# Projecting the first 128 rows un-normalised, from a copy laid out by feature, and applying the norm's factor when the result is evacuated

## The chip, the core and the metric

The kernel runs on one NeuronCore of a Trainium2 chip. The metric is the device time of one execution in microseconds (us), the median of several. The core has five engines with a queue of instructions each: PE (matrix multiply), DVE (vector), ACT (scalar and activation), POOL (GpSimd) and SP (which here only issues DMAs). An engine takes its queue strictly in order; an instruction that waits for a semaphore holds back all that stand behind it. PE writes into PSUM, which this kernel uses as eight banks of 128 x 512 floats.

## The reference, cut to what matters

Four layers, each `x += norm(mixer(norm(x)))` and then `x += norm(swiglu(norm(x)))`, over 512 prompt rows and 128 sample rows of width 1024. The change lies at the very start, in the first mixer's v projection:

```python
def rms_norm(x, g):
    y = xf * lax.rsqrt(jnp.mean(xf * xf, axis=-1, keepdims=True) + EPS)
    return (y * g.astype(jnp.float32)).astype(x.dtype)
...
hp = rms_norm(xp, norm_mix_pre[layer])
...
proj = h @ w_in
u, v, bg, cg, xb = jnp.split(proj, [...], axis=-1)
...
mu = jnp.mean(vf, axis=-1, keepdims=True)
var = jnp.mean(jnp.square(vf - mu), axis=-1, keepdims=True)
vn = ((vf - mu) * lax.rsqrt(var + EPS) * v_gain.astype(jnp.float32)).astype(v.dtype)
```

The norm of a row is one factor s for that row times a gain per feature. A product with un-normalised rows (gain applied, factor not) is therefore v / s, its mean is mu / s and its variance var / s².

## The kernel before

The 640 rows are five tiles of 128 (t = 0 to 4, here x0 to x4). All matrix products are made in split precision: an operand is a high part (ACT copies it to fp32r) and a low part (DVE subtracts the high part from it), written by `split`, and each product is three matmuls. A weight is loaded into a `raw` buffer (two buffers, two weights each) and split into a `q` tile by `operand`.

At the start `main` (L1259 on) loads x0, the gain (a broadcast to 128 partitions, L200), the first two v weights, x1, and the last two v weights. For each tile `pre_norm` (L352) squares the rows with a sum on ACT, makes mean and power −0.5 on DVE and POOL (L234), scales the rows with DVE, transposes them by eight PE transposes ("flips", L171) into two PSUM banks, and `Quarters.take` (L317) writes the splits (`x2`, `x3`, `a11`, `a12` and so on, high by ACT and low by DVE), plain copies `f` of the top half by ACT, and for the lower half a number of sums and differences, each split again. `v_proj` (L418) then makes 24 matmuls of 512 columns for each tile, in one bank `ps`, and `v_evac` in `even_mixer` (L711) evacuates it: BN_STATS, BN_AGGR, an addition, the power on POOL and one more instruction on DVE give a scale and a shift, and ACT writes the normalised rows `vn` from the bank, which is free from then on.

After the five tiles the product units (`PlainUnits`, then `Units`) start, with 320 columns a matmul and weights of their own.

A recording layer sets the order: a planner (`Weave`) runs generators by priorities and due times, a scheduler then places instructions by its own estimates, except that ACT and DVE instructions recorded while `Ordered.on` is set keep their program order. PSUM banks come from one pool of eight, in rotation: the ninth tile that is asked for waits until the first one's last reader is done.

## Time and profile before

| | |
|---|---|
| median of 3 runs | 1320.55 us (1320.53 to 1320.88) |
| the profiled execution | 1320.24 us |
| its span, first to last instruction | 1318.5 us |
| PE busy | 1294.0 us, 98% of the span |
| DVE busy | 889.0 us, 67% |
| ACT busy | 614.0 us, 47% |
| mean granted clock of PE | 0.999 |

A row of the timeline gives start and duration in us, the engine, the line, the operation, what it writes and reads, the shapes and the count of merged instructions; in brackets stands the idle time of its engine just before and what ended it. A row of the DMA view gives the transferred tile, its size and the time from issue to landing. A row of a table by windows gives the busy time of PE, PE's weight loads, DVE, ACT and POOL in that stretch, the granted clock, the DMA engines' share and GB/s.

### The profile page before, as it was taken

The page shows a single profiled execution, that of the slowest core. Times are in us where ns is not written, and L with a number is a line of the kernel's source. Part 1 is how long each engine was busy: PE and PEld are TensorE (multiplying, and loading weights), DVE is VectorE, ACT ScalarE, POOL GpSimd, SP SyncE. Part 2 cuts the span into 40 slices and gives each one's busy share as a digit, 9 for nine tenths or more (in the row PEclk, how much of TensorE's full clock was granted, in tenths as well). Part 3 has the DMA queues.
Part 4 walks back from the last instruction along what each step waited for, and adds up shares of the span by engine and source line. Part 5 has one row for each costly group of instructions (what it writes and reads, how often), then busy time and mean ns, then how long its engine had stood idle before and what let it go on. Part 6 is the DMA issues. An engine that isn't in the chain of part 4 may idle for free.

```text
span 1318.5 us, 20069 instructions
## 1 busy us (share of the span) xinstructions
PE 1294.0 (98%) x8060; PEld 1178.4 (89%) x8060; DVE 889.0 (67%) x1452; ACT 614.0 (47%) x1130; POOL 54.9 (4%) x107
## 2 busy tenths in 40 slices
PE   6999999999999999999999999999999999999997
PEld 5998989989899998998799885789999898998996
DVE  6985779837576675776736556489557575864766
ACT  5644546535254352454433455366455261551551
POOL 2200101000000000000210000010000000000000
PEclk9999999999999999999999999999999999999999
DMA  7212253212223122126435336532213021230233
GB/s 249 73 65 81 96 200 138 96 48 81 96 73 120 53 77 112 64 84 218 163 120 195 147 143 250 197 128 102 107 64 128 32 98 63 96 115 30 97 128 128
DMA packets 45965, 150.12 MB, mean 114 GB/s; under 512 B 6576, under 2 KB 8496, under 8 KB 45872
## 3 DMA queue, kind: packets, MB, share of 16 engines
q1 hardware_dynamic: 45872, 148.84, 31.2%
q8 instruction: 63, 1.03, 0.3%
q14 instruction: 30, 0.25, 0.1%
HBM read 133.57 MB, written 15.26 MB: 113 GB/s over the span
## 4 chain that ended last, share of the span: by engine, by line
PE 86%; DVE 5%; issue 3%; ACT 2%; DMA 2%; POOL 1%; SPq 0%; DVEq 0%; POOLq 0%; ACTq 0%
PE ps L167 84%; DVE t L99 3%; PE ps L171 1%; DMA xbuf<-t 1%; POOL st L234 1%; ACT t L99 1%; DMA raw<-in_dram 1%; DVE q L99 1%; ACT q L99 1%; DVE x L99 1%; DVE st L99 0%; ACT ps L99 0%; ACT f L99 0%; POOL t L751 0%; SPq L380 0%
## 5 line engine op out<-in xcount | busy, mean ns | idle before, releaser
L167 PE MATMUL ps<-x,q 128*128 128x320 f32 (+2 forms) x4884 | 727.4, 309 | 1.2 <-DVE q L99 0.8
L167 PEld LDWEIGHTS ps<-x,q 128*128 128x128 f32 x4884 | 717.5, 188 | 6.2 <-issue 2.9
L167 PE MATMUL ps<-q,hid 128*128 128x512 f32 x1800 | 417.3, 391 | 0.2 <-DVE hid L99 0.2
L99 ACT CAST q<-raw 128x1024 fp32r<-128x1024 f32 (+1 forms) x278 | 269.7, 977 | 296.8 <-PE ps L167 247.1
L99 DVE TENSOR_TENSOR q<-raw,q 128x1024 fp32r<-128x1024 f32 (+1 forms) x278 | 313.9, 1132 | 134.4 <-ACT q L99 129.3
L167 PEld LDWEIGHTS ps<-q,hid 128*128 128x128 f32 x1800 | 335.5, 188 | 70.9 <-issue 1.7
L99 ACT COPY t<-ps 128x320 f32<-128x320 f32 (+2 forms) x304 | 135.0, 451 | 193.7 <-PE ps L167 173.8
L99 DVE TENSOR_TENSOR t<-ps,t 128x512 f32<-128x512 f32 (+2 forms) x164 | 100.3, 614 | 93.2 <-PE ps L167 93.0
L99 DVE TENSOR_TENSOR raw<-raw 128x512 f32<-128x512 f32 (+1 forms) x141 | 121.9, 866 | 11.6 <-DMA raw<-in_dram 10.0
L99 DVE TENSOR_TENSOR t<-t,t 128x512 f32<-128x512 f32 (+4 forms) x107 | 57.8, 551 | 48.5 <-ACT t L99 46.7
L234 POOL TENSOR_TENSOR st<-st,mhalf 128x1 f32<-128x1 f32 x45 | 31.7, 705 | 1005.9 <-DVE st L99 1001.1
L99 DVE SCALAR_TENSOR_TENSOR t<-t,st,t 128x512 f32<-128x512 f32 (+1 forms) x60 | 54.5, 925 | 16.6 <-POOL st L234 15.1
L99 ACT ACTIVATE t<-t 128x320 f32<-128x320 f32 (+1 forms) x60 | 40.1, 668 | 45.0 <-issue 26.2
L171 PE MATMUL ps<-ident,t 128*128 128x128 f32 x288 | 42.2, 281 | 12.0 <-DVE t L99 9.6
L171 PEld LDWEIGHTS ps<-ident,t 128*128 128x128 f32 x288 | 33.4, 143 | 21.9 <-DVE t L99 9.9
L99 ACT CAST hid<-t 128x320 fp32r<-128x320 f32 (+1 forms) x96 | 45.9, 482 | 11.1 <-DVE t L99 8.9
L99 DVE TENSOR_TENSOR t<-t 128x320 f32<-128x320 f32 (+3 forms) x90 | 48.8, 542 | 1.4
L99 DVE TENSOR_TENSOR hid<-t,hid 128x320 fp32r<-128x320 f32 (+1 forms) x96 | 48.8, 512 | 0.1
L167 PE MATMUL ps<-q,x 128*128 128x512 f32 x192 | 47.6, 402 | 1.2 <-DVE st L99 0.8
L99 ACT ACTIVATE ps<-t 128x512 f32<-128x512 f32 x40 | 24.1, 603 | 50.6 <-DVE t L99 50.6
L167 PEld LDWEIGHTS ps<-q,x 128*128 128x128 f32 x192 | 36.1, 192 | 10.6 <-DVE q L99 2.3
L99 DVE TENSOR_TENSOR t<-t,ps 128x320 f32<-128x320 f32 x47 | 22.9, 487 | 33.2 <-PE ps L167 33.2
(90 smaller groups left out, 497.5 us busy)
## 6 DMA issues: line engine op xcount, KB each, us to landing
raw<-in_dram SPq DMA_DIRECT2D x184, 512.0 KB, 4.1
x<-in_dram SPq DMA_DIRECT2D x24, 512.0 KB, 6.1
t<-in_dram SPq DMA_DIRECT2D x22, 512.0 KB, 5.8
xbuf<-t SPq DMA_DIRECT2D x15, 512.0 KB, 3.4
t<-xbuf SPq DMA_DIRECT2D x15, 512.0 KB, 3.9
out_dram<-t SPq DMA_DIRECT2D x15, 256.0 KB, 2.0
c<-in_dram SPq DMA_DIRECT2D x4, 512.0 KB, 4.2
fscr<-x SPq DMA_DIRECT2D x2, 768.0 KB, 3.3
```

What stands on the lines that cost most here:

```text
L99: ins = op(*args, **kw)
L167: nc.tensor.matmul(out, lhsT=lhsT, rhs=rhs, start=start, stop=stop, skip_group_check=more)
L171: nc.tensor.transpose(out=out, in_=in_, identity=ident)
L234: nc.gpsimd.tensor_tensor(out=r, in0=ms, in1=mhalf, op=ALU.pow)
```

## The change

A copy of the first 128 rows laid out by feature (`first_t`: 128 features by 8 by 128 rows) and the gain as a column per feature (`first_g`) become inputs of the program. The first tile's product no longer waits for its norm or its flips: half of the copy is multiplied by the gain on DVE, half on POOL, both halves are split into two `top` tiles, and `v_proj` multiplies these for t = 0. `v_evac` multiplies the variance by s² and the scale by s for t = 0. Tile x0 is still loaded, normed, transposed and taken, since later units read it, but after x1. The loads are put in another order, and the due times of the tiles' later steps change.

```diff
-    def pre_norm(t, x, X, wait, xn=None):
+    def pre_norm(t, x, X, wait, xn=None, scale=None, pause=False):
...
             r = norm.get()
+            if scale is not None:
+                scale.append(r)
+        if pause:
+            yield
+        with tc.high_priority():
             dve.scalar_tensor_tensor(out=xn, in0=x, scalar=r, in1=X.gain, op0=ALU.mult, op1=ALU.mult)
...
-    def v_proj(X, hls, evac):
+    def v_proj(X, hls, evac, first=None):
...
-                x = X.rows(k, t)
+                if t or first is None:
+                    x = X.rows(k, t)
+                else:
+                    x = [f[:, k, :] for f in first]
...
+            var = mv[:, 1:2]
+            if t == 0:
+                var = st()
+                dve.tensor_scalar(
+                    out=var, in0=mv[:, 1:2], scalar1=scale[0], scalar2=scale[0], op0=ALU.mult, op1=ALU.mult
+                )
...
             r = rsqrt(ve)
+            if t == 0:
+                own, r = r, st()
+                dve.tensor_tensor(out=r, in0=own, in1=scale[0], op=ALU.mult)
...
-        load(0)
-        X.gain = bcast(g_mix_pre[0], D, t4)
-        w = [next(feed) for _ in range(2)]
+        gt = cst.tile([P, NK], F32, name="gt")
+        xt0 = t4([P, NK, P])
+        nc.sync.dma_start(out=xt0[:, :HK], in_=first_t[:, :HK])
+        nc.sync.dma_start(out=gt, in_=first_g)
+        w = [next(feed)]
+        nc.sync.dma_start(out=xt0[:, HK:], in_=first_t[:, HK:])
+        w.append(next(feed))
+        xt.append(None)
         load(1)
         w += [next(feed) for _ in range(2)]
-        first = pre_norm(0, xt[0], X, 0)
+        X.gain = bcast(g_mix_pre[0], D, t4)
+        xt[0] = t4([P, D])
+        nc.sync.dma_start(out=xt[0], in_=in_row(0))
+        top = [hidp.tile([P, NK, P], F32R, tag="hid", name=nm("top")) for _ in range(2)]
+        hls = []
+        for i in range(2):
+            c = slice(i * HK, (i + 1) * HK)
+            (nc.gpsimd if i else dve).tensor_tensor(
+                out=xt0[:, c], in0=xt0[:, c], in1=gt[:, c].unsqueeze(2).broadcast_to([P, HK, P]), op=ALU.mult
+            )
+        for i in range(2):
+            c = slice(i * HK, (i + 1) * HK)
+            split((top[0][:, c], top[1][:, c]), xt0[:, c])
+            hls.append(operand(w[i]))
+        second = pre_norm(1, xt[1], X, A1 + 3000, pause=True)
+        next(second)
+        hls += [operand(w[2]), operand(w[3])]
+        next(second)
+        W.spawn(second, 0, A1 + 3000)
+        scale = []
+        first = pre_norm(0, xt[0], X, 0, None, scale)
         next(first)
-        hls = [operand(w[0])]
-        for _ in first:
-            pass
-        W.signal(X.top[0])
-        hls.append(operand(w[1]))
-        start(1, A1)
-        hls += [operand(w[2]), operand(w[3])]
+        W.spawn(first, 0, 2 * A2 - 500)
         for t in range(2, TT):
             load(t)
-            start(t, A1 + (t - 1) * A2)
+            start(t, A1 + t * A2 - 500)
```

Three places of the resulting order follow; a row's number of a buffer tells two of one name apart. First SP, the loads at the start. Before (`t4_13` is x0, `t4_14` the gain, `raw15` and `raw17` the v weights, `t4_16` x1, `raw103` the first unit's weights, `t4_32` x2):

```order
L1271 DMA t4_13_104<-in_0_dram 128x1024
L200 DMA t4_14_106<-in_6_dram 128x1024
L214 DMA raw15_108<-in_13_dram 128x1024
L216 DMA raw15_108<-in_13_dram 128x1024
L1271 DMA t4_16_111<-in_0_dram 128x1024
L214 DMA raw17_113<-in_13_dram 128x1024
L216 DMA raw17_113<-in_13_dram 128x1024
```

Now (`t4_13` is the copy by feature in two halves, `gt` the gain's column, `t4_15` x1, `t4_17` the gain, `t4_18` x0):

```order
L1302 DMA t4_13_105<-in_27_dram 128x512
L1303 DMA gt_104<-in_28_dram 128x8
L216 DMA raw14_108<-in_13_dram 128x1024
L218 DMA raw14_108<-in_13_dram 128x1024
L1305 DMA t4_13_105<-in_27_dram 128x512
L1292 DMA t4_15_112<-in_0_dram 128x1024
L216 DMA raw16_114<-in_13_dram 128x1024
L218 DMA raw16_114<-in_13_dram 128x1024
L202 DMA t4_17_117<-in_6_dram 128x1024
L1312 DMA t4_18_119<-in_0_dram 128x1024
```

The gain and x0 have moved from the head of the queue to its ninth and tenth place; behind them stand three small loads, one weight and x2.

Second PE, from the end of the second v tile to the third. Before (`ps66` is the bank of v tile 1, `t4_38` the normed x3, `ps74` v tile 2):

```order
L167 MATMUL ps66_291<-q31_157,x3_94 128x512 x6
L171 MATMUL ps67_316<-ident_84,t4_38_172 128x128 [waits DVE_49,PE_49]
L171 MATMUL ps67_316<-ident_84,t4_38_172 128x128 x3
L171 MATMUL ps68_321<-ident_84,t4_38_172 128x128 [waits PE_49]
L171 MATMUL ps68_321<-ident_84,t4_38_172 128x128 x3
L167 MATMUL ps74_337<-q22_124,q1_92 128x512 [waits Activation_49]
L167 MATMUL ps74_337<-q22_124,q1_92 128x512 x5
```

Now (`ps63` is v tile 1, `t4_39` the normed x3, `ps83` v tile 2):

```order
L169 MATMUL ps63_251<-q28_145,x3_94 128x512 x6
L173 MATMUL ps77_344<-ident_84,t4_39_169 128x128 [waits Activation_49]
L173 MATMUL ps77_344<-ident_84,t4_39_169 128x128 x3
L173 MATMUL ps78_349<-ident_84,t4_39_169 128x128 [waits PE_49,Activation_49]
L173 MATMUL ps78_349<-ident_84,t4_39_169 128x128 x3
L169 MATMUL ps83_375<-q21_127,q1_92 128x512 [waits PE_49,Activation_49]
L169 MATMUL ps83_375<-q21_127,q1_92 128x512 x5
```

The flips of x3 now take the ninth and tenth bank, and wait for ACT: the ninth is the bank of v tile 0 again, the tenth that of x1's first flips.

Third ACT, the same stretch. Before (`vn47` is the evacuation of v tile 0, the rows with `f` the plain copies):

```order
L99 COPY f12_103<-ps54_216 128x4x128
L99 ACTIVATE t4_38_172,st39_173<-t4_37_170 128x1024
L99 CAST q1_92<-ps61_255 128x512
L99 CAST x2_93<-ps60_250 128x4x64
L99 CAST x3_94<-ps61_255 128x4x64
L99 COPY f11_102<-ps60_250 128x4x64
L99 ACTIVATE t4_43_182,st44_183<-t4_42_180 128x1024
L99 COPY f12_103<-ps61_255 128x4x64
L99 CAST x4_95<-ps61_255 128x4x64
L99 CAST x4_95<-ps68_321 128x4x128
L99 ACTIVATE vn47_190<-ps52_198,st59_247,st58_245 128x512
```

Now (`t4_39` and `t4_44` are the squares of x3 and x4, `vn48` the evacuation of v tile 0, whose bank is `ps53`):

```order
L99 CAST q1_92<-ps67_279 128x512
L99 ACTIVATE t4_39_169,st40_170<-t4_38_167 128x1024
L99 CAST x2_93<-ps66_274 128x4x64
L99 CAST x3_94<-ps67_279 128x4x64
L99 ACTIVATE t4_44_179,st45_180<-t4_43_177 128x1024
L99 ACTIVATE vn48_187<-ps53_195,st62_242,st61_240 128x512
L99 COPY f11_102<-ps54_220 128x4x128
L99 COPY f12_103<-ps55_225 128x4x128
L99 COPY f11_102<-ps64_264 128x4x128
L99 COPY f12_103<-ps65_269 128x4x128
L99 COPY f11_102<-ps66_274 128x4x64
L99 COPY f12_103<-ps67_279 128x4x64
```

All plain copies `f` of x1, x0 and x2 have moved behind the evacuation of v tile 0. On DVE that evacuation's BN_STATS stands, as before, behind the low parts of x2, two differences of a unit's raw weights and the mean of x4, and BN_AGGR behind the scaling of x4.

## The prediction

> **What bounds the kernel now.** I read the page's busy shares first, then a table by windows of the first 50 us, then the timeline there. In the windows' rows the columns are PE, PE's weight loads, DVE, ACT, POOL, the granted clock, the DMA share and GB/s.

> ```profile
> PE 1294.0 (98%) x8060; PEld 1178.4 (89%) x8060; DVE 889.0 (67%) x1452; ACT 614.0 (47%) x1130; POOL 54.9 (4%) x107
> PE   6999999999999999999999999999999999999997
> 0.00:8.00 8.00, 0.00 (x0) 0.00 (x0) 1.69 (x3) 2.49 (x4) 1.38 (x9) 1.00 0.75 247
> 35.00:40.00 5.00, 5.00 (x24) 4.14 (x23) 5.00 (x12) 3.53 (x8) 0.00 (x0) 1.00 0.00 0
> 40.00:45.00 5.00, 5.00 (x24) 4.14 (x23) 5.00 (x9) 4.18 (x7) 0.00 (x0) 1.00 0.00 0
> ```

> PE is the bound almost everywhere; its first slice of 33 us is the only weak one before the last. So any time that PE loses or gains at the start stays in the total. From 35 to 45 us DVE is busy without a gap too: this stage has two engines at their limit, and what is put later on DVE can reach PE.

> ```profile
> 8.04 1.97 PE L171 MATMUL ps<-ident,t 128*128 128x128 f32 x8 [8.04 <-DVE t L99]
> 9.83 3.04 PE L167 MATMUL ps<-q,x 128*128 128x512 f32 x6
> 17.48 2.79 PE L167 MATMUL ps<-q,x 128*128 128x512 f32 x11
> 21.47 5.71 PE L167 MATMUL ps<-q,x 128*128 128x512 f32 x24
> 27.03 1.03 PE L171 MATMUL ps<-ident,t 128*128 128x128 f32 x8
> 34.89 2.89 PE L167 MATMUL ps<-q,a 128*128 128x512 f32 x12
> 45.77 7.20 PE L167 MATMUL ps<-x,q 128*128 128x320 f32 x48
> ```

> PE does nothing for 8.04 us (load, square, power, scaling of x0), makes its first matmul at 9.83, ends v tile 0 at about 20.2 and v tile 1 at 27.0. It starts the flips of x3 at 27.03, v tile 3 at 34.89 and the units at 45.77.

> ```profile
> 28.06 0.69 DVE L99 BATCH_NORM_STATS2 st<-ps 128x6 f32<-128x512 f32 x1
> 30.02 0.17 DVE L99 BATCH_NORM_AGGREGATE st<-st 128x2 f32<-128x6 f32 x1
> 30.71 0.54 POOL L234 TENSOR_TENSOR st<-st,mhalf 128x1 f32<-128x1 f32 x1
> 31.29 0.16 DVE L99 SCALAR_TENSOR_TENSOR st<-st,st 128x1 f32<-128x1 f32 x1
> 31.48 0.78 ACT L99 ACTIVATE vn<-ps,st,st 128x512 f32<-128x512 f32 x1 [2.51 <-DVE st L99]
> 32.31 0.66 PE L171 MATMUL ps<-ident,t 128*128 128x128 f32 x4 [0.38 <-ACT vn L99]
> ```

> The evacuation of v tile 0 is late already: its product is done at 20, but its BN_STATS stands on DVE behind other work and runs at 28.06; ACT frees the bank at 32.26. Only the last four flips of x4 needed that bank, so PE waited 0.38.

> **The change, step by step.** *PE's start.* The first product needs the first half of the copy, its gain, one split and one weight, and no flips. Its end still hangs on the last v weight.

> ```profile
> 3.15 0.44 SPq L214 DMA_DIRECT2D raw<-in_dram  x1
> 3.63 0.57 SPq L216 DMA_DIRECT2D raw<-in_dram  x1
> raw<-in_dram SPq DMA_DIRECT2D x1, 512.0 KB, 8.6
> raw<-in_dram SPq DMA_DIRECT2D x1, 512.0 KB, 9.6
> 13.96 1.98 ACT L99 CAST q<-raw 128x1024 fp32r<-128x1024 f32 x2
> 42.84 1.19 DVE L99 TENSOR_TENSOR q<-raw,q 128x1024 fp32r<-128x1024 f32 x1
> ```

> The last two v weights land at 3.15 + 8.6 = 11.8 and 3.63 + 9.6 = 13.2, 1.4 apart; 512 KB take about 1.3 in the full queue. Seven loads of 512 KB are through at 13.2. Now the gain and x0 come behind the weights, so weights land some 2.5 earlier (10.9 for the last), and the four splits follow each other on ACT and DVE, about 1.2 each. I put v tile 0's last matmul at 16.1 instead of 20.2: PE is 4 us ahead there, but without the flips of x1.

> *POOL's multiplication* (128 x 512) has no row of its kind. Below stands a POOL memset of this size, 0.53; above, four selections of 128 x 128, 1.03 together, or with the slowest single row of that kind four times some 4 us. I take 1.1, by the selections. It starts when the copy's second half lands, near 7.1, and ACT, which casts the second half next, then waits until about 8.2. Up to 1.5 costs nothing, since x0's landing (below) holds the chain; beyond that it delays tile 0's end and the rest by the same amount.

> ```profile
> 24.20 0.53 POOL L745 MEMSET t<- 128x512 f32 x1
> 33.06 1.03 POOL L751 TENSOR_SCALAR_AFFINE_SELECT t<-t 128x128 f32<-128x128 f32 x4
> ```

> [...]

> *x0 moves from first to tenth in the queue*, and with it the chain square, mean, power, scaling. Now ahead of it stand the seven loads of before less x0, the two halves of the copy and one tiny load: 13.2 + 1.3 (the halves are 512 KB together, and x0 itself takes the place of x0) + 0.1 = 14.6. The three small loads behind it take 0.5: the last of them, `hist`, landed at 6.58 + 7.1 = 13.7, 0.5 after the last weight. That row, and the durations of the chain:

> ```profile
> 6.58 0.33 SPq L765 DMA_DIRECT2D hist<-in_dram  x1
> hist<-in_dram SPq DMA_DIRECT2D x1, 32.0 KB, 7.1
> 15.85 1.06 ACT L99 ACTIVATE t<-t 128x1024 f32<-128x1024 f32 x1
> 16.81 0.19 ACT L99 ACTIVATION_READ_ACCUMULATOR t<-t 128x1 f32 x1
> 18.47 0.15 DVE L99 TENSOR_SCALAR st<-st 128x1 f32<-128x1 f32 x1
> 18.70 0.55 POOL L234 TENSOR_TENSOR st<-st,mhalf 128x1 f32<-128x1 f32 x1 [3.73 <-DVE st L99]
> 19.28 1.28 DVE L99 SCALAR_TENSOR_TENSOR t<-t,st,t 128x1024 f32<-128x1024 f32 x1
> 40.34 1.89 DVE L99 TENSOR_TENSOR x<-t,x 128x512 fp32r<-128x512 f32 x3
> 36.54 1.42 DVE L99 TENSOR_TENSOR x<-t,x 128x256 fp32r<-128x256 f32 x4
> 10.88 1.18 ACT L99 COPY f<-ps 128x512 f32<-128x512 f32 x2 [0.25 <-DVE x L99]
> 16.34 1.09 PE L171 MATMUL ps<-ident,t 128*128 128x128 f32 x8 [0.38 <-DVE t L99]
> ```

> x0: 14.6, ACT 1.25, DVE 0.15, POOL 0.55, DVE 1.28, with handovers: its scaling ends at 18.0. On DVE the low parts of x1 stand behind it, so PE's second v tile runs from 18.7, with the flips of x0 and x2 between: 22 matmuls of 0.227 (5.71 / 24 is 0.238 with its tail, 12 take 2.72 from start to start) and 13 flips of 0.11, so **v tile 1 ends at 25.1**, 1.9 earlier than before.

> *Then the wait.* In the order now, the flips of x3 are the ninth taker of a bank, and wait for ACT's `vn` of tile 0, with whose bank they begin. Follow its chain. x2 lands behind x0, the small loads and a weight: 14.6 + 0.5 + 1.3 + 1.3 = 17.7; x3 and x4, at 1.3 a load, near 21.6 and 24.3, before ACT gets to them. Square to 19.0, mean behind x1's low parts at 19.3, power 19.9, scaling 21.3, flips (behind PE's tile) 22.6. ACT now casts four pieces and squares x3: 24.6. Mean and power to 25.4, scaling of x3 26.7. DVE then has four entries ahead of the statistics (two of 128 x 256, two of 128 x 512, 2.0 together) and x4's mean: BN_STATS at 28.7, the scaling of x4 1.3, BN_AGGR, the new multiplication by s² and the addition 0.5, power 0.55, the new multiplication by s and the shift 0.4: 32.2. ACT 0.78: **33.0**. So the evacuation comes 0.8 later than before (32.26), where the two new small instructions are 0.3, but PE now needs it for the flips of x3. It waits from 25.1 to 33.0, 7.9 us, and starts them 6.0 later than the 27.03 of before.

> *What follows.* x3's flips, v tile 2 and x4's flips are 16 x 0.11 + 24 x 0.227 = 7.2 of PE, where before 27.03 to 34.89 took 7.9: v tile 3 starts at 40.3, 5.4 late. Behind `vn` ACT has six copies (four of 0.5, two of 0.3) and one cast: DVE gets its first piece of the lower half at 35.9 and has, up to the low part of the first unit's weight, 37 instructions: 20 of 128 x 512 at 0.61 from start to start, 10 of 128 x 256 at 0.35, one of 1.15, two BN_STATS of 0.6 and four small ones: 18.7, so 54.6. In the order of before this weight was split at 42.84, ahead of x4's pieces; now behind most of them. PE meets this twice: in v tile 4 it waits about 1.3 for a low part (until 47.0), ends it at 52.0, makes ten matmuls of the units (1.5) and waits again, from 53.5 to 54.7. Before, ten such matmuls after 45.77 ended at 47.2. **The start loses 7.5.**

> *Later.* In three places DVE's order differs by a few entries (the entry into each feed-forward block, and the odd mixer). Each moves one scaling (1.28 for 1024 columns) past a few others; in the two entries the later order seems to hold PE by up to one such entry. I take 0.5 each, +1.0; bounds are -1 and +2. The new small instructions and the two inputs cost nothing elsewhere.

> Sum: +7.5 + 1.0 = +8.5. The profiled execution took 1320.24, 0.3 below the median of 1320.55, so **1328.7**.

> **Rivals.** *The evacuation is in time.* If ACT's `vn` came before 25.1, PE would keep its 1.9 at v tile 1, or 4 if tile 1 kept up with tile 0: 1318.4 or 1316. For it speaks that tile 0's product ends at 16. Against it: the order puts BN_STATS behind x4's mean, and x4 cannot land before x2 (17.7). It decides at 25.1. Chance 5%, of which 3% end over 0.2% faster.

> *PE is slow after its idle time.* Its first eight flips took 1.97, eight at 16.34 took 1.09; the page shows no second such restart, since PE is busy for 90% or more of every later slice but the last; now there is a gap of 8. If PE is at half speed for 4 us of work after 33.0, it loses 2.2, and the two waits for DVE (1.3 and 1.2) absorb this: 1329. If it is slow for 6, or POOL's multiplication takes 3, 1 to 2 more are lost: 1330 to 1333. Chance 14%. [...]

> *A smaller loss.*

> ```profile
> 4.11 1.06 ACT L99 ACTIVATE t<-t 128x1024 f32<-128x1024 f32 x1 [2.03 <-DMA t<-in_dram]
> 6.70 1.28 DVE L99 SCALAR_TENSOR_TENSOR t<-t,st,t 128x1024 f32<-128x1024 f32 x1 [1.26 <-DMA t<-in_dram]
> ```

> The gain's broadcast is slower than other loads: x0's landing released ACT at 4.1, the gain's released DVE at 6.7, some 2.5 for 512 KB. If it took 1.3 in its new place, x0 and all behind it would be up to 1.2 earlier; with the later places at -1 this gives 1325. Chance 7%.

> *Nothing changes.* Were tile 0 still held by x0's norm, the start would be late and no bank short: 1320. The order excludes nearly all of it: 2%.

> **How the numbers follow.** The forecast itself has 72%. A measurement tells about 0.2%, 2.6 us, from no change. Faster 3%; same 4% (the 2% above and the other 2% of the evacuation in time); slower 93%. The range takes the smaller loss at its middle and the slow restart nearly whole: 1325.5 to 1332.5.

> **What would show it.** PE's first matmul near 6.3; x0's square near 14.7; v tile 1 done near 25; then one idle time of PE near 8 us, ended by ACT's `vn`, with `vn` near 32.3 to 33.0; DVE without a gap from 36 to 55; the units' bulk near 54.7. A PE without that gap makes the prediction wrong; flips of over 0.2 each after it would show the slow clock; a start that loses 7.5 with another total puts the error into the later order.

## The result, and the profile after

The changed kernel took **1332.64 us** in the median (1332.38 to 1332.88, four runs), the kernel before 1320.62 beside it (1320.53 to 1320.88): a ratio of 1.009, 95% interval 1.0075 to 1.0105. It is 12.0 us slower. The forecast was slower by 8.5, and the time lies 0.14 above the end of its range. The span of the profiled execution grew from 1318.5 to 1331.0, by 12.5; the places of the loss below are read from these two profiles.

PE's rows of the changed kernel's timeline: v tile 0's last 17 matmuls, x1's flips, the end of v tile 1, the flips of x3, v tile 2, the start of v tile 3, the first four matmuls of the units and their bulk.

```profile
12.78 5.79 PE L169 MATMUL ps<-q,top 128*128 128x512 f32 x17 [0.46 <-DVE st L99]
18.41 1.03 PE L173 MATMUL ps<-ident,t 128*128 128x128 f32 x8
...
24.47 2.75 PE L169 MATMUL ps<-q,x 128*128 128x512 f32 x11
35.05 1.97 PE L173 MATMUL ps<-ident,t 128*128 128x128 f32 x8 [7.83 <-ACT vn L99]
36.68 7.38 PE L169 MATMUL ps<-q,q 128*128 128x512 f32 x24
...
44.68 3.01 PE L169 MATMUL ps<-q,a 128*128 128x512 f32 x12
...
55.69 0.74 PE L169 MATMUL ps<-x,q 128*128 128x320 f32 x4
...
56.86 5.44 PE L169 MATMUL ps<-x,q 128*128 128x320 f32 x36
```

The mark of the forecast is there: one idle time of 7.83 (forecast 7.9), ended by ACT's `vn`. But it begins and ends 2 us later than forecast (27.2 to 35.05, not 25.1 to 33.0). The units start at 55.69, 9.92 later than the 45.77 of before.

The chain to the evacuation, and DVE behind it, in the same timeline:

```profile
8.76 1.11 POOL L1317 TENSOR_TENSOR t<-t,gt 128x512 f32<-128x512 f32 x1 [7.30 <-DMA t<-in_dram]
...
15.38 1.06 ACT L99 ACTIVATE t<-t 128x1024 f32<-128x1024 f32 x1 [0.97 <-DMA t<-in_dram]
...
30.54 0.69 DVE L99 BATCH_NORM_STATS2 st<-ps 128x6 f32<-128x512 f32 x1
...
34.22 0.78 ACT L99 ACTIVATE vn<-ps,st,st 128x512 f32<-128x512 f32 x1 [6.20 <-DVE st L99]
...
37.79 0.42 DVE L99 TENSOR_TENSOR a<-ps,a 128x256 fp32r<-128x256 f32 x1 [1.63 <-ACT a L99]
...
44.09 0.70 DVE L99 BATCH_NORM_STATS2 st<-ps 128x6 f32<-128x512 f32 x1 [0.36 <-PE ps L169]
...
55.72 1.19 DVE L99 TENSOR_TENSOR q<-raw,q 128x1024 fp32r<-128x1024 f32 x1
```

DVE gets its first lower half at 37.79 and ends the low part of the first unit's weight at 56.91. PE has no wait from 35.05 to its bulk. The first matmul of the units that waits for DVE's semaphore, the eleventh (third of the row at 56.86), starts at 57.15, 0.25 after that weight is ready.

The rest of the loss comes far behind the start. The same 24 matmuls at the entries into the two feed-forward blocks, in the kernel before and then in the changed one:

```profile
214.14 3.78 PE L167 MATMUL ps<-x,q 128*128 128x320 f32 x24 [0.43 <-DVE q L99]
...
889.47 3.80 PE L167 MATMUL ps<-x,q 128*128 128x320 f32 x24 [0.38 <-DVE q L99]
```

```profile
225.43 3.78 PE L169 MATMUL ps<-x,q 128*128 128x320 f32 x24 [1.46 <-DVE q L99]
...
902.12 3.78 PE L169 MATMUL ps<-x,q 128*128 128x320 f32 x24 [1.46 <-DVE q L99]
```

At both, PE waits about one us longer for the low part of a weight. It is 11.29 late at the first and 12.65 at the second, and that stays. So 9.9 are lost at the start and 2.7 later, where the forecast had 7.5 and 1.0. Of the 2.7 the two longer waits are 1.0 and 1.1; the rest are smaller delays around them.

PE's clock, by a table by windows of the changed kernel (the columns are PE, weight loads, DVE, ACT, POOL, granted clock, DMA share, GB/s):

```profile
26.56:29.97 3.41, 0.67 (x3) 0.20 (x2) 2.71 (x6) 1.46 (x4) 1.02 (x2) 1.00 0.02 2
29.97:33.38 3.41, 0.00 (x0) 0.00 (x0) 3.07 (x7) 0.00 (x0) 2.64 (x6) 0.50 0.08 7
33.38:36.80 3.42, 1.75 (x9) 1.75 (x9) 1.49 (x6) 2.58 (x6) 1.88 (x6) 0.50 0.25 80
36.80:40.21 3.41, 3.41 (x10) 2.67 (x9) 1.90 (x5) 3.15 (x9) 0.09 (x1) 0.50 0.02 5
```

In the gap the granted clock falls to 0.50, at 29.97, and it is 1.00 again at 40.21. In this time the flips of x3 took 1.97 instead of 1.03, and v tile 2, half in it, 7.38, where 24 such matmuls took 5.71 before: the case of the second rival.

### The profile page after: what moved, and what is told of

Read it like the earlier page. It is cut to its first block, busy times and chain, and to the rows that moved or that the text cites. A ratio compares the mean times of both kernels' runs of the same rounds, so it can differ in the third digit from the quotient of the medians.

```text
span 1331.0 us, 20104 instructions
## 1 busy us (share of the span) xinstructions
PE 1298.2 (98%) x8060; PEld 1181.0 (89%) x8060; DVE 892.9 (67%) x1457; ACT 614.6 (46%) x1132; POOL 56.7 (4%) x108
## 3 DMA queue, kind: packets, MB, share of 16 engines
q8 instruction: 63, 1.03, 0.3%
## 4 chain that ended last, share of the span: by engine, by line
PE 85%; DVE 5%; issue 3%; DMA 3%; POOL 2%; ACT 1%; SPq 0%; POOLq 0%; DVEq 0%; ACTq 0%
PE ps L169 84%; DVE t L99 4%; PE ps L173 2%; POOL st L236 1%; DMA xbuf<-t 1%; ACT t L99 1%; DMA t<-in_dram 1%; DMA raw<-in_dram 1%; DVE q L99 0%; DVE st L99 0%; DVE x L99 0%; DMA x<-in_dram 0%; ACT q L99 0%; ACT ps L99 0%; ACT x L99 0%
## 5 line engine op out<-in xcount | busy, mean ns | idle before, releaser
L99 ACT CAST q<-raw 128x1024 fp32r<-128x1024 f32 (+1 forms) x278 | 269.7, 977 | 300.2 <-PE ps L169 249.2
L99 DVE TENSOR_TENSOR q<-raw,q 128x1024 fp32r<-128x1024 f32 (+1 forms) x278 | 313.9, 1132 | 136.0 <-ACT q L99 130.9
L99 ACT COPY t<-ps 128x320 f32<-128x320 f32 (+2 forms) x304 | 135.2, 451 | 194.6 <-PE ps L169 175.7
L99 DVE TENSOR_TENSOR t<-ps,t 128x512 f32<-128x512 f32 (+2 forms) x164 | 100.3, 614 | 96.4 <-PE ps L169 95.8
L99 DVE TENSOR_TENSOR raw<-raw 128x512 f32<-128x512 f32 (+1 forms) x141 | 121.8, 865 | 10.7 <-DMA raw<-in_dram 8.5
L99 DVE TENSOR_TENSOR t<-t,t 128x512 f32<-128x512 f32 (+4 forms) x107 | 57.7, 551 | 48.6 <-ACT t L99 46.5
L99 DVE SCALAR_TENSOR_TENSOR t<-t,st,t 128x512 f32<-128x512 f32 (+1 forms) x60 | 54.7, 927 | 18.9 <-POOL st L236 18.4
L99 ACT ACTIVATE t<-t 128x320 f32<-128x320 f32 (+1 forms) x60 | 40.1, 669 | 45.5 <-issue 29.9
L99 ACT CAST hid<-t 128x320 fp32r<-128x320 f32 (+1 forms) x96 | 45.9, 482 | 11.0 <-DVE t L99 8.8
L173 PEld LDWEIGHTS ps<-ident,t 128*128 128x128 f32 x288 | 33.3, 143 | 19.9 <-ACT vn L99 8.2
L99 DVE TENSOR_TENSOR t<-t 128x320 f32<-128x320 f32 (+3 forms) x90 | 48.8, 543 | 1.4
L99 DVE TENSOR_TENSOR hid<-t,hid 128x320 fp32r<-128x320 f32 (+1 forms) x96 | 48.8, 512 | 0.1
L99 ACT ACTIVATE ps<-t 128x512 f32<-128x512 f32 x40 | 24.1, 602 | 52.6 <-DVE t L99 52.6
L99 DVE TENSOR_TENSOR t<-t,ps 128x320 f32<-128x320 f32 x47 | 22.9, 487 | 32.5 <-PE ps L169 32.5
L169 PE MATMUL ps<-q,x 128*128 128x512 f32 x168 | 40.8, 395 | 0.9 <-DVE q L99 0.7
L99 ACT ACTIVATE t<-ps,st 128x512 f32<-128x512 f32 (+4 forms) x48 | 24.5, 513 | 36.8 <-DVE st L99 31.9
## 6 DMA issues: line engine op xcount, KB each, us to landing
raw<-in_dram SPq DMA_DIRECT2D x184, 512.0 KB, 4.1
x<-in_dram SPq DMA_DIRECT2D x24, 512.0 KB, 6.9
t<-in_dram SPq DMA_DIRECT2D x22, 512.0 KB, 6.5
xbuf<-t SPq DMA_DIRECT2D x15, 512.0 KB, 2.9
t<-xbuf SPq DMA_DIRECT2D x15, 512.0 KB, 4.1
c<-in_dram SPq DMA_DIRECT2D x4, 512.0 KB, 4.0
```

Of the source, the lines that this page charges most:

```text
L99: ins = op(*args, **kw)
L169: nc.tensor.matmul(out, lhsT=lhsT, rhs=rhs, start=start, stop=stop, skip_group_check=more)
L173: nc.tensor.transpose(out=out, in_=in_, identity=ident)
```

## The experiments

### The loss after the start: one priority block made two

The diff closes the high-priority block in `pre_norm` ahead of the scaling and opens it again, so that `pause` can stand between. Every later caller of `pre_norm` gets two blocks as well. First that edit alone, in the kernel before:

```diff
             r = norm.get()
+        with tc.high_priority():
             dve.scalar_tensor_tensor(out=xn, in0=x, scalar=r, in1=X.gain, op0=ALU.mult, op1=ALU.mult)
```

> The kernel before, with one difference: the norm's high-priority block in pre_norm, which holds the square, the mean, the power and the scaling, is closed ahead of the scaling and opened again for it, as the change does for its pause. Nothing of the un-normalised product is in it. Theory A (this edit alone makes the loss after the start): DVE's order differs only at the entries into the two feed-forward blocks and in the odd mixer, as it does in the changed kernel; PE is on time up to 203 us of the kernel before, loses 1.2 to 1.6 at each of the two entries, and the total is 1322.6 to 1323.6. Theory B (the loss after the start comes from other buffers or from the late start itself): within 0.4 of 1320.7.

Measured: 1323.45 (1322.74 to 1324.92) against 1320.74, ratio 1.0021 (1.0012 to 1.0029). DVE at the first entry, the kernel before and then this one (`q` is the awaited low part):

```profile
208.81 0.68 DVE L99 TENSOR_TENSOR t<-t,t 128x512 f32<-128x512 f32 x1
209.40 1.28 DVE L99 SCALAR_TENSOR_TENSOR t<-t,st,t 128x1024 f32<-128x1024 f32 x1
...
211.59 0.68 DVE L99 TENSOR_TENSOR t<-t,t 128x512 f32<-128x512 f32 x1
...
212.87 1.22 DVE L99 TENSOR_TENSOR q<-raw,q 128x1024 fp32r<-128x1024 f32 x1
```

```profile
210.26 1.28 DVE L99 SCALAR_TENSOR_TENSOR t<-t,st,t 128x1024 f32<-128x1024 f32 x1 [0.40 <-POOL st L234]
...
212.12 1.28 DVE L99 TENSOR_TENSOR t<-t,t 128x512 f32<-128x512 f32 x2
...
214.06 1.22 DVE L99 TENSOR_TENSOR q<-raw,q 128x1024 fp32r<-128x1024 f32 x1
```

A multiplication by the gain that filled DVE's wait for the power now stands behind the scaling, DVE idles 0.40, and the low part of the weight comes 1.2 later. Theory A holds. Now the reverse, the changed kernel with the scaling back in one block for all tiles but x1:

```diff
+            if not pause:
+                dve.scalar_tensor_tensor(out=xn, in0=x, scalar=r, in1=X.gain, op0=ALU.mult, op1=ALU.mult)
         if pause:
             yield
-        with tc.high_priority():
-            dve.scalar_tensor_tensor(out=xn, in0=x, scalar=r, in1=X.gain, op0=ALU.mult, op1=ALU.mult)
+            with tc.high_priority():
+                dve.scalar_tensor_tensor(out=xn, in0=x, scalar=r, in1=X.gain, op0=ALU.mult, op1=ALU.mult)
```

> The changed kernel, with the scaling back inside the norm's high-priority block for every tile but x1 (the only one that uses the pause). Theory A: the loss after the start, 2.75 in the changed kernel (PE is 9.92 late at the units and 12.67 late at the end), goes as a whole; the start stays at 9.9; the total is 1332.64 - 2.75 = 1329.9, within 0.5. Theory B: within 0.4 of 1332.6.

Measured: 1330.06 (1329.79 to 1331.03), ratio 1.0071 (1.0059 to 1.0084). The wait at the first entry is 0.44 again, and at the second 0.41:

```profile
223.40 3.80 PE L169 MATMUL ps<-x,q 128*128 128x320 f32 x24 [0.44 <-DVE q L99]
```

The loss at the two entries is this edit, shown from both sides, and it has nothing to do with the un-normalised product. In this profile the units start at 54.96, 0.7 earlier than in the changed kernel, since the v weights landed earlier, and PE loses 0.6 near 800 us where the changed kernel loses almost nothing; so the 2.6 between the two medians cannot be told off place by place.

### The loss at the start: due times or product

The changed kernel with early due times, and the kernel before with the late ones:

```diff
-        W.spawn(second, 0, A1 + 3000)
+        W.spawn(second, 0, 2000)
-        W.spawn(first, 0, 2 * A2 - 500)
+        W.spawn(first, 0, 2000)
-            start(t, A1 + t * A2 - 500)
+            start(t, A1 + (t - 1) * A2)
```

> The changed kernel with one difference: the due times of the tiles' flips and splits are put back to early ones (x1 and x0 at 2000, x2 to x4 at 2000 + (t - 1) * 5000, as the kernel before has them for x2 to x4). In the order this moves ACT's plain copies of x1's and x0's flips ahead of the evacuation of v tile 0, so the flips of x3 take x1's banks and no longer that of v tile 0. Theory A (PE waits only for a bank, and the slow clock follows from that wait): the flips of x3 start when x3 is scaled, 27.29 + 1.28 = 28.6 in the changed kernel's timeline, not at 35.05; PE has no idle time above 3 us and no stretch at clock 0.5 after the first 17 us. The start then loses about 1.5 to 2 against the kernel before (28.6 against 27.03), and with the 2.0 lost later the total is 1323.5 to 1325. Theory B (the time hangs on x0's late chain and on DVE's and ACT's work, and the bank is only where it shows): the flips of x3 may start early, but the units start 7 or more late all the same, and the total stays at 1329 or above.

```diff
-        start(1, A1)
+        start(1, A1 + 3000)
-            start(t, A1 + (t - 1) * A2)
+            start(t, A1 + t * A2 - 500)
```

> The kernel before, with x0 first and its product from the normed rows, and only the due times of the change: x1 due 3000 later, x2 to x4 4500 later. Theory A (the due times alone set much of the loss, since they put the splits of the tiles' lower halves late on DVE and ACT): slower by 3 to 6, 1323.5 to 1326.5, with a new wait of PE for DVE near the start of the units. Theory B (the loss comes from the copy and from x0's late place in the queue): within 0.5 of 1320.6.

Measured: 1326.95 (1326.28 to 1327.46), ratio 1.0046 (1.0031 to 1.0061), and 1324.01 (1322.77 to 1324.75), ratio 1.0023 (1.0013 to 1.0032). With early due times:

```profile
29.28 1.74 PE L173 MATMUL ps<-ident,t 128*128 128x128 f32 x8 [2.23 <-DVE t L99]
...
49.09 7.20 PE L169 MATMUL ps<-x,q 128*128 128x320 f32 x48
```

The wait for the bank is gone, and the units start at 49.09, 3.3 late instead of 9.9. Theory A was right in kind, but 2 too low: PE now waits 2.23 for x3's scaling, behind this wait too the clock was 0.50, for 3.41 us (29.51 to 32.92), and the later loss was 2.9. The late due times in the kernel before:

```profile
45.05 0.74 PE L167 MATMUL ps<-x,q 128*128 128x320 f32 x4
...
49.66 6.71 PE L167 MATMUL ps<-x,q 128*128 128x320 f32 x44 [2.69 <-DVE q L99]
```

PE is at the units 0.7 earlier than the 45.77 of the kernel before and after twelve matmuls waits 2.69 for the first unit's weight, whose low part stands behind the tiles' lower halves. Theory A holds. About 2.2 are lost there; the profiled run is the fastest of ten (1322.77). By the medians the due times cost 3.3 without any change of the product, and 5.7 with it (1332.64 less 1326.95).

Then the changed kernel with v tile 0 and its evacuation recorded early (`v_proj` is called once for tile 0 and once for the others, and the three steps below are tile 0's; the buffer of the evacuation's gain moves behind them):

```diff
+        em = even_mixer(X, hls, top, scale)
+        for _ in range(3):
+            next(em)
         for t in range(2, TT):
...
-        X = yield from even_mixer(X, hls, top, scale)
+        X = yield from em
```

> The changed kernel, with v tile 0 and its evacuation recorded ahead of the tiles x2 to x4, and everything else as it is, the late due times too. On DVE the statistics of v tile 0 then stand ahead of x1's low parts, and on ACT the evacuation ahead of the square of x2. Theory A (bank only): the wait of 7.83 us ahead of x3's flips is gone, they start near 28.6, the clock stays at full speed, and the total is 1323.5 to 1325.5. Theory B (late due times also leave DVE's work on the lower halves late, so that a wait for DVE takes the place of the wait for the bank): the flips of x3 start near 28.6, but PE meets one or two new waits of 2 to 4 us for a low part or a weight of the units, and the total is 1328 to 1331.

Measured: 1330.74 (1330.48 to 1331.23), ratio 1.0074 (1.0057 to 1.0091).

```profile
24.21 0.78 ACT L99 ACTIVATE vn<-ps,st,st 128x512 f32<-128x512 f32 x1 [1.35 <-DVE st L99]
...
31.30 0.85 PE L173 MATMUL ps<-ident,t 128*128 128x128 f32 x6 [0.61 <-DVE t L99]
...
47.48 3.36 PE L169 MATMUL ps<-q,a 128*128 128x512 f32 x10 [2.98 <-DVE a L99]
```

The first row is of ACT: `vn` comes at 24.21, and no flips wait for a bank. Those of x3 start at 31.30, when x3 is scaled, later than the 28.6 that both theories had; and in v tile 4 PE waits 2.98 for a low part. Theory B holds: taking away the wait alone brings back only 1.9 of 12, because behind it DVE's work on the lower halves is as late.

### The clock

Filling PE's gap: 36 products of a zero matrix with 32 columns of the identity, added to v tile 1's bank.

```diff
+            for _ in range(36 if t == 1 and first else 0):
+                nc.tensor.matmul(ps[:, :32], lhsT=zero, rhs=ident[:, :32], start=False, stop=False, skip_group_check=True)
             evac(t, ps)
```

> The changed kernel with 36 additional matmuls of 128 x 32 that add zero to the bank of v tile 1, right behind its product; DVE and ACT have the same order as in the changed kernel, and the result is unchanged. They are meant to keep PE busy in its idle time of 7.83 us, if one takes about 0.2 us. Theory A (the slow clock is on the path): the clock stays at 1.0 after 17 us, x3's flips start at 35.05 as before but take 1.1 instead of 1.97, v tile 2 takes 5.7 instead of 7.38, and the total falls by 1 to 2.5, to 1330.1 to 1331.6. Theory B (the forecast's: two waits for DVE absorb what the slow clock loses): the same stretch is quicker, PE waits for DVE in v tile 4 or at the first unit instead, and the total stays within 0.4 of 1332.6. Were the matmuls much shorter than 0.2 us, the clock would fall all the same and the run would tell nothing of its price.

Measured: 1337.33 (1334.12 to 1337.36), ratio 1.0119 (1.0103 to 1.0134).

```profile
26.71 12.10 PE L445 MATMUL ps<-ident,zero 128*128 128x32 f32 x72
38.62 1.95 PE L173 MATMUL ps<-ident,t 128*128 128x128 f32 x8
```

```profile
26.93:30.34 3.41, 3.41 (x33) 3.41 (x32) 3.37 (x7) 0.74 (x2) 0.45 (x1) 1.00 0.05 7
30.34:43.99 13.65, 13.65 (x58) 12.88 (x58) 6.45 (x18) 6.19 (x15) 4.63 (x11) 0.50 0.08 22
```

Each was two instructions of 0.168: 12.1 in all, 3.6 too long. And though PE's rows have no gap, the clock was 0.50 all the same, from 30.34 to 43.99. The run tells nothing of the price, as its expectation allows for.

Filling PE's first idle time: 28 flips of the identity into v tile 0's bank, in the changed kernel and then in the kernel before (there in the bank of x0's flips).

```diff
+            for i in range(28 if t == 0 and first else 0):
+                nc.tensor.transpose(out=ps[:, i % 4 * P : (i % 4 + 1) * P], in_=ident, identity=ident)
             for k in range(NK):
```

> The changed kernel, with 28 additional flips of the identity matrix into the bank of v tile 0 ahead of its product (they are overwritten; at 0.25 each they fill about 7 us in which PE has nothing to do). DVE and ACT keep their order. Theory A (PE's half speed until 16.32 makes v tile 0 late, and with it the flips of x1 and all behind them): the clock is at 1.0 before 13 us, v tile 0 ends near 16.7 instead of 18.3, the flips of x1 start when x1 is scaled (15.77 + 1.28 = 17.1) instead of at 18.41, the evacuation ends 0.8 to 1.3 earlier than 35.0, and the total is 1331.3 to 1331.9. Theory B (the late landings of the weights and of x0 set the chain): the flips of x1 may start early, but the evacuation of v tile 0 stays at 35.0 within 0.3 and the total within 0.4 of 1332.6.

> The kernel before, with the same 28 additional flips of the identity ahead of x0's flips, in the bank that these overwrite; DVE and ACT keep their order. Theory A (the slow clock at the start holds this kernel too): the flips of x0 take 1.1 instead of 1.97 and the first six matmuls 1.4 instead of 3.0, and 0.5 to 1 of it reaches the end: 1319.7 to 1320.2, the only version so far below the kernel before. Theory B (v tile 0 waits for its weights, which end its waits at 13.06, 14.32 and 16.34 whatever PE's clock): those three waits grow by what the matmuls lose, v tile 1 ends at 27.0 as before, and the total stays within 0.3 of 1320.7.

Measured: 1332.46 (1331.89 to 1333.04), ratio 1.0088 (1.0074 to 1.0101), and 1320.9 (1320.13 to 1323.21), ratio 1.0003 (0.9994 to 1.0012). In the changed kernel the clock was full from 7.64 to 31.53, and:

```profile
15.07 2.79 PE L169 MATMUL ps<-q,top 128*128 128x512 f32 x11 [0.32 <-DVE q L99]
17.70 1.03 PE L173 MATMUL ps<-ident,t 128*128 128x128 f32 x8
...
34.46 1.97 PE L173 MATMUL ps<-ident,t 128*128 128x128 f32 x8 [7.67 <-ACT vn L99]
...
43.06 0.69 DVE L99 BATCH_NORM_STATS2 st<-ps 128x6 f32<-128x512 f32 x1
...
54.48 0.74 PE L169 MATMUL ps<-x,q 128*128 128x320 f32 x4
...
54.55 1.19 DVE L99 TENSOR_TENSOR q<-raw,q 128x1024 fp32r<-128x1024 f32 x1
```

Neither theory fits as a whole. The flips of x1 came 0.7 earlier (A had 1.3), the evacuation 0.6 earlier, the units 1.2 earlier (54.48 instead of 55.69); but at the first output projection PE waits for ACT and DVE in this run, and 0.2 of it was left behind that:

```profile
184.81 0.73 PE L169 MATMUL ps<-q,hid 128*128 128x512 f32 x2 [0.72 <-ACT hid L99]
185.87 2.33 PE L169 MATMUL ps<-q,hid 128*128 128x512 f32 x9 [0.32 <-DVE hid L99]
```

The changed kernel has the row of 185.87 at 186.03. The total did not move (B). But the chain at this projection comes from the load of a weight, for which ACT's cast waits 3.90; it landed 8.2 us after its issue, 7.4 in the changed kernel, 8.0 in the run of all three below and 7.2 to 7.7 in the other profiles. Why it was slower is open, so the run does not show that an earlier start is worth nothing: the 0.7 by which the run with one block was early at the units was still there behind the projection. In the kernel before, the first flips took 1.09 instead of 1.97 and nothing came of it, as theory B has it; but in that run the clock was 0.50 again from 14.88 to 18.29.

The changed kernel's run with flips also prices the slow clock behind the gap. Here it lasted from 31.53 to 38.36, 6.83 instead of 10.24; but most of what is missing fell into PE's idle time, and behind PE's restart it was 3.90 (34.46 to 38.36) instead of 5.16 (35.05 to 40.21). At a clock of 0.50 these 1.26 us less are 0.63 of PE's work, and from its restart to the units' first matmul PE took 20.0 instead of 20.6: all of it came back. DVE was quicker by as much: from its first lower half to the end of the first unit's weight it took 18.5 (37.20 to 55.74) instead of 19.1, and the row at 43.06 has no wait for PE where the changed kernel had 0.36. More could hardly come back: the eleventh matmul of the units starts at 55.94, 0.2 after DVE's end. So of the 2.6 of work that half clock took from PE in the changed kernel, some 0.6 to 0.8 reached the units, an estimate from these two runs.

### All three together

Early due times, one block, and the flips at the start.

> Three of these edits together: the early due times, the scaling inside the priority block, and the additional flips at the start. If the three losses are independent, it is the run with early due times, 1326.95, less 2.9 (what that run lost after its start) and less 0 to 1.5 for the clock: 1322.5 to 1324. It would be below the kernel before only if the un-normalised product gained something by itself, which needs v tile 1 done clearly before 27 us and the flips of x3 before 27.0. A theory that the un-normalised product gains 2 us or more once the order is right expects 1318.7 or less.

Measured: 1324.69 (1323.31 to 1325.73), ratio 1.0028 (1.0018 to 1.0038).

```profile
28.71 1.06 PE L173 MATMUL ps<-ident,t 128*128 128x128 f32 x8 [2.23 <-DVE t L99]
...
47.52 7.20 PE L169 MATMUL ps<-x,q 128*128 128x320 f32 x48
```

The median is 0.7 above what was expected; its profiled run (1323.3), the fastest of eight, lies inside. At the first output projection it loses 0.7, with the slow load named above. With the due times and the block put back the change still gains nothing: the flips of x3 wait for its scaling until 28.71, where the kernel before starts them at 27.03. x2 and x3 land at 18.25 and 22.12 here, at 14.62 and 20.40 in the kernel before. Whether these loads or the order on ACT and DVE hold the scaling was not separated, so the cause of the last 4.0 us is open in part. No version tried beats the kernel before.

## Why the prediction was right in kind and too low

| step | forecast | measured |
|---|---|---|
| first matmul | 6.3 | 7.77 |
| POOL's multiplication | 1.1, from 7.1 | 1.11, from 8.76 |
| x0 landed | 14.6 | 15.4 |
| v tile 0 ends | 16.1 | 18.4 |
| v tile 1 ends | 25.1 | 27.2 |
| `vn` ends | 33.0 | 35.0 |
| PE's idle time | 7.9 | 7.83 |
| v tile 3 starts | 40.3 | 44.68 |
| wait in v tile 4 | 1.3 | none |
| wait at the first unit | 1.2 | none |
| units' bulk, eleventh matmul | 54.7 | 57.15 |
| lost at the start | 7.5 | 9.9 |
| lost later | 1.0 | 2.7 |

**The mechanism was right up to PE's restart.** PE waited for the bank of v tile 0, for as long as forecast. Behind that DVE did take as long as forecast, 19.1 instead of 18.7 from its first lower half to the first unit's weight, but PE's two waits for it, 2.5 together, did not come. In their place PE lost 2.6 to the half clock and needed the weight 0.25 after DVE had ended it. That the two sizes are so close is chance.

**The step that failed is the sum, in both of its terms**: the start was put at +7.5 and measured 9.9, the later order at +1.0 and measured 2.7. One of them alone would have left the time inside the range (1331.1 with 9.9, 1330.4 with 2.7, by the same working); both together give 1332.8, and the profiled run took 1332.75.

**The later order**: "in the two entries the later order seems to hold PE by up to one such entry. I take 0.5 each, +1.0; bounds are -1 and +2." It cost 2.7, above its own upper bound. I had seen that the order differs at these places, but not that PE waits there in the kernel before already (0.43 and 0.38 for the weight's low part), so that each delay of DVE counts in full, nor that the cause stands in the diff: the second `with tc.high_priority()`.

**The start** was too small by 2.4. "I put v tile 0's last matmul at 16.1" priced its matmuls at full speed. The last 17 took 5.79, where 17 of 0.227 are 3.9, since PE was at half speed until 16.32, where the records of the granted clock begin (six such matmuls took 3.29 from 9.03, and 1.67 from 13.08 in the run with the flips at the start); and the loads came 0.8 (x0) to 1.7 (the copy's second half, at POOL) later than forecast. As x1's flips stand behind v tile 0 on PE, the whole chain to `vn` moved by 2.0. Two runs divide this in part. With the flips at the start the clock was full and x1's flips came 0.7 earlier, though the last v weight landed at 12.96 instead of 12.56. With one block they came 0.7 earlier too (17.71), at half speed until 15.56 (six took 3.42 from 8.19), and there that weight landed at 11.94. So the slow clock and the late loads each hold this stage by some 0.7; the rest was not separated. The other 0.4 lies behind the gap: from its restart to the eleventh matmul of the units PE took 22.1, forecast 21.7.

**The rivals.** *PE is slow after its idle time* came true: 10.24 us of half clock, 5.2 of them after the restart. What it said of the price held in the main: it took the place of the two waits for DVE, and by the estimate above 0.6 to 0.8 of its 2.6 reached the units. *The evacuation is in time* was given 1318.4 if `vn` came before 25.1. In the run with an early evacuation it ended at 24.99, and the time was 1330.74: this rival left out that the scaling of x3 and DVE's lower halves are next. *A smaller loss*, through a faster gain, did not come; x0 landed later, not earlier. POOL's multiplication was taken rightly.

## What to carry to other kernels

Look in a diff for edits that reach further than their purpose: a block closed and opened again for one tile's sake cost 2.6 to 2.7 us, most of it in two places some 200 and 900 us on, and was to be found by asking of every changed helper who else calls it. Before taking a wait away, ask which engine is late next: here the bank, the scaling of x3 and DVE's lower halves stood one behind the other, and removing one gave 1.9 of 12. And price the matmuls of a kernel's first microseconds by rows from before the clock rises (here 17 took 5.79, reckoned at 3.9).

## What the runs showed of the hardware

```profile
26.10:29.51 3.41, 1.18 (x7) 0.70 (x6) 2.72 (x6) 2.09 (x7) 1.42 (x2) 1.00 0.02 8
```

```profile
45.60:49.01 3.41, 1.53 (x7) 1.27 (x8) 3.34 (x8) 2.11 (x4) 0.55 (x1) 1.00 0.00 0
```

```profile
11.47:14.88 3.41, 1.70 (x7) 0.85 (x6) 1.29 (x3) 3.41 (x6) 0.55 (x1) 1.00 0.66 228
```

```profile
4.64:8.05 3.41, 1.74 (x16) 1.51 (x15) 1.44 (x2) 0.92 (x3) 0.55 (x1) 1.00 1.00 353
```

```profile
44.70:48.12 3.42, 2.27 (x15) 1.93 (x13) 3.39 (x6) 2.22 (x5) 0.00 (x0) 1.00 0.00 0
48.12:51.53 3.41, 1.86 (x13) 1.87 (x14) 3.29 (x6) 0.62 (x1) 1.11 (x1) 1.00 0.00 0
```

So the clock fell behind a wait of 2.23 (early due times) and behind two of 0.96 and 0.76 (flips in the kernel before), and not behind one of 2.69 (late due times in the kernel before), which lay in two pieces, busy for 2.27 and 1.86. The wait of 2.23 in the run of all three left the clock alone; its piece, from 27.14 to 30.55 (counted from the 6.66 below), had 1.83.

**Rows without a gap, and the clock fell.** In the filled gap narrow matmuls of 32 columns kept PE's rows busy for 3.41 of 3.41 (26.93 to 30.34), and the clock was 0.50 from 30.34. Their matrix was zero; whether the width or the zeros did it was not tried. Flips of 128 columns went with an early rise: in three runs 28 of them ran from 1.5 on, and the clock was full at 4.64, 6.66 and 7.64 (the nine from 5.63 took 1.66 in the second and 2.13 in the third), where without them it was full at 12.63 in the kernel before and at 16.32 in the changed kernel. In the kernel before with flips, the first of the three, nothing but these ran on PE until 7.96:

```profile
1.51 4.78 PE L366 MATMUL ps<-ident 128*128 128x128 f32 x28 [1.51 <-POOL ident masks.py:199]
```
